# Three more seven-product pairs, and weight sums made in HBM by DMAs, in a two-layer decoder trunk

## The chip, the cores and the metric

The kernel runs on one core of a Trainium2 chip. The time is device microseconds of one execution; the median of several is compared. A core has TensorE (PE; its weight loads are listed apart as PEld), VectorE (DVE), ScalarE (ACT), GpSimd (POOL) and SyncE (SP), which work side by side and wait for each other through semaphores. Loads and stores are DMAs; SP, ACT and POOL can issue them.

## The reference

Two layers on x of 512 tokens by 1024 features, all in float32:

```python
h = rmsnorm(x, g_mix)
aq, ak, av, rq, rk, rv, rg, ga, gb = split(h @ w_in)     # 5888 columns
ya = sliding_window_sink_attention(rope(aq), rope(ak), av, sinks) @ w_a
r = chunkwise_retention(rotate(rq), rotate(rk), rv)
r = r * rsqrt(mean(r * r) + EPS) * silu(rg)              # per head
mixed = sigmoid(ga) * ya + sigmoid(gb) * (r @ w_b)
x = x + mixed @ w_out
x = x + square(relu(rmsnorm(x, g_mlp) @ w_up)) @ w_down  # 1024 -> 4096 -> 1024
```

After both layers a final RMSNorm gives the output. The inputs are drawn at random with fixed seeds.

## The kernel before, in words

**Products.** Activations lie transposed, 128 features by 512 tokens, and each float32 operand is held as a high part and a low part (`split`, L336). A product is three matmuls: high by high, high by low, low by high (L332 to L334). A "chunk" is 128 output features of all tokens; over 1024 input features it takes 8 x 3 = 24 matmuls of 512 columns.

**Weights** come in units of 128 x 1024 in the order of `unit_order` (L59). For each, SP loads the raw unit (`load_until`, L186), ACT copies its high part (L286), DVE takes the low part by subtraction (L287). There are three buffers for raw units and three each for high and low parts; unit i+2 is split when unit i is taken up (`unit`, L292), and loads run some three units ahead of that.

**Pairs.** Two output chunks can be made together in seven products of half the tokens instead of eight (Strassen's scheme in Winograd's form; `narrow_pair`, L629, and, with two of three matmuls merged, `wide_pair`, L1327). A pair is four "parts", each at the size of a unit, that hold the two halves of the weights and four sums of them (S1 to S3 and the like, `add_part`, L248). The activations need four sums as well, the "forms" (`sum_input`, L594: four sums and two splits for each half of the features). A narrow pair works with 256 columns, its three accumulators are copied or joined by ACT and DVE (L640 to L661), and the `step` argument lets other work be placed between its products. In this kernel pairs are w_b 0 and 2 (retention output), w_out 2, 4 and 6, and all of w_up from unit 4 on; w_down is plain, in twos (`two_chunks`, L406), and its last quarter is a `group` of four chunks (L387) and four single chunks (L1446 to L1451).

**Sums of the weights.** For most pairs DVE makes them in place, 4 x 128x512, when the part is due. For the five pairs of `PARKED` (L54) they are made earlier in the same layer, beside w_in's value projection: `raws_ahead` (L230) loads both units, `sums_ahead` (L237) adds and stores four sums to HBM, and `load_part` (L211) later loads the parts ready-made. A pair loads 1 MB when DVE makes the sums and 1.75 MB when they are parked.

**Order.** The code gives each engine's order as a priority; the framework's list scheduler then places ready work first, so that TensorE's order of units can differ a little from the code's. SP and POOL work off their DMAs in the order given.

**Around the change.** In the MLP (`mlp_sequence`, L82), two w_down chunks alternate with one w_up pair. After layer 0's last chunk, `put_down(c, True)` (L1414) adds to x, splits the new input for layer 1 (L342, L343), adds its squares (L425, L426) and stores x to `spill`. Layer 1's first group of w_in begins at once; after its first unit the squares' sum is prepared (L435, L436, L339, L340), and after its second unit TensorE sums them over features and ACT and DVE make the reciprocal RMS (L474 to L477). In the retention output, `mixed_pair` (L1218) multiplies a pair with its gate; chunks 4 to 7 go through `put_mixed` (L1195). `silu` (L976) is a Sigmoid on ACT and a product on DVE; around it ACT also makes Sigmoid gates (L904, L1124) and square roots (L451, L476).

Of the kernel before, what the change touches and what calls it, by code (L numbers as in the profile page):

```python
# [18 lines left out]
P = 128  # L19
T = 512  # L20
# [33 lines left out]
PARKED = (("w_b", 0), ("w_b", 2), ("w_out", 6), ("w_up", 4), ("w_up", 6))  # L54
# [4 lines left out]
def unit_order():  # L59
# [68 lines left out]
def decoder(ctx, tc, xT, x_first, w_in, w_a, w_b, w_out, w_up, w_down, tables, decay, band, triangles, g_last, out):  # L128
# [37 lines left out]
    order = [(layer, *u) for layer in range(DEPTH) for u in unit_order()]  # L166
# [19 lines left out]
    def load_until(n):  # L186
        while state["loaded"] < min(n, len(order)):
# [4 lines left out]
            else:  # L192
                raws[i] = raw_tile()
                for at in halves(i):
                    queue = nc.scalar if i == 0 and at.start == 0 else nc.sync
                    queue.dma_start(raws[i][:, at], weights[name][layer, j][:, at])
                    if i < 3:
                        load_x()
            state["loaded"] += 1

# [5 lines left out]
    park = {at: dram.tile([P, 4, T], F32, name="park_%s_%d" % at) for at in PARKED}  # L206

    def is_parked(i):
        return order[i][1] == "pair" and (order[i][4], order[i][2]) in park

    def load_part(i):  # L211
        layer, _, j, part, src = order[i]
        one, two = (weights[src][layer, j + a] for a in range(2))
        if is_parked(i):
            sums = park[src, j]
            raws[i] = raw_tile()
            sides = ((one[:, LEFT], sums[:, 0, :]), (sums[:, 1, :], one[:, RIGHT]), (sums[:, 2, :], sums[:, 3, :]), (two[:, LEFT],))
            for side, part_of in zip((LEFT, RIGHT), sides[part]):
                nc.sync.dma_start(raws[i][:, side], part_of)
# [17 lines left out]
    def sums_ahead(src, j, two):  # L237
# [4 lines left out]
        nc.vector.tensor_tensor(w2[:, RIGHT], w1[:, LEFT], w2[:, RIGHT], ALU.subtract)  # L242
        nc.vector.tensor_tensor(w1[:, LEFT], s1, w1[:, LEFT], ALU.subtract)
        nc.vector.tensor_tensor(w1[:, RIGHT], w1[:, RIGHT], w1[:, LEFT], ALU.subtract)
        for n, part in enumerate((s1, w1[:, LEFT], w2[:, RIGHT], w1[:, RIGHT])):
            nc.sync.dma_start(park[src, j][:, n, :], part)

    def add_part(i):  # L248
# [4 lines left out]
        elif part == 1:  # L253
            w1 = raws[i - 1]
            nc.vector.tensor_tensor(raws[i][:, LEFT], w1[:, RIGHT], w1[:, LEFT], ALU.subtract)
        elif part == 2:
            raws[i] = big("raw3").rearrange("p a t -> p (a t)")
            w1, w2, z2 = raws[i - 2], raws[i + 1], raws[i - 1]
            nc.vector.tensor_tensor(raws[i][:, LEFT], w1[:, LEFT], w2[:, RIGHT], ALU.subtract)
            nc.vector.tensor_tensor(raws[i][:, RIGHT], z2[:, RIGHT], z2[:, LEFT], ALU.subtract)  # L260
# [320 lines left out]
    def layer_body(layer):  # L581
# [12 lines left out]
        def sum_input(by_form, b, ks):  # L594
# [11 lines left out]
            split(*parts_of_forms(0), f[0].rearrange("p (j k) t -> p j k t", k=2))  # L606
            nc.vector.tensor_tensor(t3, b22, b12, ALU.subtract)
            nc.vector.tensor_tensor(t4, b21, t2, ALU.subtract)
# [20 lines left out]
        def narrow_pair(pool, step, form, block, put):  # L629
# [23 lines left out]
            ins = nc.vector.tensor_tensor(z[:, 1, SECOND], b, eu[:, :H], ALU.add).ins  # L653
# [7 lines left out]
            put(1, FIRST, b, z)  # L661
# [314 lines left out]
        def silu(i):  # L976
            s = temp("sig")
            nc.scalar.activation(s, rg[i], AF.Sigmoid)
            nc.vector.tensor_tensor(rg[i], rg[i], s, ALU.mult)
# [132 lines left out]
        to_load, to_sum = [(layer, *at) for at in PARKED], []  # L1112

        def load_ahead():
            if to_load:
                to_sum.append((*to_load[0][1:], raws_ahead(*to_load.pop(0))))
# [101 lines left out]
        def mixed_pair(c):  # L1218
# [4 lines left out]
            def put(i, at, src, z):  # L1223
# [10 lines left out]
        for c in (0, 2):  # L1234
            mixed_pair(c)
        all_of(delayed)
# [3 lines left out]
        homes_m = [forms_home(), None, forms_home(), None]  # L1240
        by_form_m = [h and h[1] for h in homes_m]
        sum_input(by_form_m, gate_tiles[:2], 0)
        for c in range(4, KD):
# [29 lines left out]
        def add_to_x(c):  # L1273
            def put(i, at, src, z):
                own = x[:, c + i, at] if isinstance(i, int) else x[:, c : c + 2, at]
                return nc.vector.tensor_tensor(own, own, src, ALU.add)
# [21 lines left out]
        def positive(i, at, src, z):  # L1298
# [3 lines left out]
            return nc.vector.scalar_tensor_tensor(z[:, i, at], src, 0.0, factor, ALU.max, ALU.mult)  # L1302
# [5 lines left out]
        up = [[] for _ in range(4)]  # L1308
        up_slots = [[] for _ in range(4)]
# [329 lines left out]
```

## Time and profile before

| | |
|---|---|
| median of 3 runs | 1473.33 us (1473.19 to 1473.95) |
| the profiled execution | 1473.8 us |
| its span, first to last instruction | 1472.0 us |
| moved by DMA | 194.45 MB, mean 132 GB/s |
| read from HBM, written to HBM | 171.63 MB, 18.89 MB |

A busy time is the union of an engine's instructions; matmuls overlap in the pipeline, so their own durations are longer than the distance between their starts. A row of instructions gives its start and its length in us, engine, line, operation and tiles (out<-in), the shape, how many it merges (x), and in brackets what the engine waited for before it. A row of a group gives the count, then busy us and mean ns, then the engine's idle time before. A row of DMAs gives the count, KB each and the median us from issue to landing. "L333" is line 333.

### The profile page before, as it was taken

To read this page: it belongs to the slowest core of one execution; us is meant where nothing else is said; L and a number is where in the kernel's file an instruction comes from. 1 tells how busy PE (TensorE), PEld (TensorE's weight loads), DVE (VectorE), ACT (ScalarE), POOL (GpSimd) and SP (SyncE) were. 2 spreads that over 40 slices of the span, in tenths; PEclk is the share of its full clock that TensorE was granted. 3 is DMA by queue.
4 is the path that set the end of the run, shared out by engine and by line. 5 is a ranking of instruction groups with operands and counts; after the bars stand their busy time and mean duration, and the time that the engine had idled before them with its cause. 6 is when DMAs were issued, how large, how long until landed. Compare 5 with 4: busy or idle time off the path is not lost.

```text
span 1472.0 us, 20220 instructions
## 1 busy us (share of the span) xinstructions
PE 1464.8 (100%) x7466; PEld 1249.6 (85%) x7466; DVE 1166.7 (79%) x1920; ACT 810.9 (55%) x1306; POOL 3.8 (0%) x14
## 2 busy tenths in 40 slices
PE   9999999999999999999999999999999999999998
PEld 7888888888988888888888888888989888888887
DVE  7998878778988787776678986786899877878763
ACT  7656356654684445444455753656547754444553
POOL 0000000000000000000000000000000000000000
PEclk9999999999999999999999999999999999999999
DMA  6422843356443332333543258333654522333241
GB/s 227 127 89 92 300 158 99 102 172 212 126 126 118 101 115 93 104 104 115 165 126 97 86 186 272 104 104 102 207 171 126 154 95 93 114 106 109 90 140 57
DMA packets 71043, 194.45 MB, mean 132 GB/s; under 512 B 8457, under 2 KB 8609, under 8 KB 70945
## 3 DMA queue, kind: packets, MB, share of 16 engines
q1 hardware_dynamic: 70656, 192.65, 40.7%
q8 instruction: 58, 0.95, 0.3%
q10 hardware_dynamic: 288, 0.52, 0.1%
q14 instruction: 41, 0.33, 0.1%
HBM read 171.63 MB, written 18.89 MB: 129 GB/s over the span
## 4 chain that ended last, share of the span: by engine, by line
PE 94%; issue 5%; DMA 1%; DVE 0%; ACT 0%; POOLq 0%; DVEq 0%; SPq 0%
PE mm L334 22%; PE mm L332 22%; PE mm L333 22%; PE mm L1336 11%; PE mm L1337 5%; PE rv L332 2%; PE rv L333 2%; PE rv L334 2%; PE score L842 1%; PE r L332 1%; PE r L334 1%; PE r L333 1%; PE pT L797 0%; PE pv L823 0%; PE pv L824 0%
## 5 line engine op out<-in xcount | busy, mean ns | idle before, releaser
L333 PE MATMUL mm<-r,hi 128*128 128x512 f32 (+1 forms) x1568 | 572.5, 367 | 0.0
L332 PE MATMUL mm<-r,hi 128*128 128x512 f32 (+1 forms) x1568 | 569.7, 367 | 0.6 <-ACT r L342 0.6
L334 PE MATMUL mm<-r,lo 128*128 128x512 f32 (+1 forms) x1568 | 563.9, 367 | 0.2
L286 ACT ACTIVATE hi<-raw 128x1024 fp32r<-128x1024 f32 (+1 forms) x334 | 334.1, 1002 | 386.4 <-PE mm L333 206.8
L287 DVE TENSOR_TENSOR lo<-raw,hi 128x512 fp32r<-128x512 f32 (+1 forms) x335 | 384.7, 1151 | 111.6 <-ACT hi L286 107.9
L334 PEld LDWEIGHTS mm<-r,lo 128*128 128x128 f32 x1568 | 293.7, 188 | 48.7 <-DVE lo L287 1.4
L332 PEld LDWEIGHTS mm<-r,hi 128*128 128x128 f32 x1568 | 293.8, 188 | 47.5 <-ACT r L342 1.4
L333 PEld LDWEIGHTS mm<-r,hi 128*128 128x128 f32 x1568 | 294.3, 188 | 45.9
L1336 PE MATMUL mm<-r,hi 128*128 128x512 f32 x728 | 252.1, 391 | 0.0
L1337 PE MATMUL mm<-r,lo 128*128 128x256 f32 x728 | 200.5, 277 | 0.0
L1336 PEld LDWEIGHTS mm<-r,hi 128*128 128x128 f32 x728 | 136.5, 188 | 28.6
L1337 PEld LDWEIGHTS mm<-r,lo 128*128 128x128 f32 x728 | 136.7, 188 | 3.1 <-DVE lo L287 0.7
L1416 DVE TENSOR_TENSOR x<-x,mm 128x512 f32<-128x512 f32 x56 | 37.8, 686 | 28.9 <-PE mm L334 28.9
L1409 ACT ACTIVATE z<-z 128x512 f32<-128x512 f32 x56 | 32.4, 623 | 48.7 <-DVE z L1389 48.7
L333 PE MATMUL rv<-lo,r 128*128 128x512 f32 x128 | 49.8, 389 | 0.0
L334 PE MATMUL rv<-hi,r 128*128 128x512 f32 x128 | 49.5, 389 | 0.0
L332 PE MATMUL rv<-hi,r 128*128 128x512 f32 x128 | 49.4, 390 | 0.0
L340 DVE TENSOR_TENSOR r<-z,r 128x512 fp32r<-128x512 f32 x64 | 42.9, 686 | 3.0 <-ACT r L339 2.6
L339 ACT ACTIVATE r<-z 128x512 fp32r<-128x512 f32 x64 | 38.4, 619 | 7.9 <-DVE z L1070 7.8
L869 ACT ACTIVATE sm<-sm,st 128x256 f32<-128x256 f32 (+1 forms) x64 | 30.1, 472 | 18.9 <-DVE st L857 18.7
L1389 DVE SCALAR_TENSOR_TENSOR z<-z,rstd 128x512 f32<-128x512 f32 x52 | 35.7, 687 | 0.6
L340 DVE TENSOR_TENSOR r<-sums,r 128x1024 fp32r<-128x1024 f32 x24 | 28.9, 1220 | 0.0
(273 smaller groups left out, 1693.0 us busy)
## 6 DMA issues: line engine op xcount, KB each, us to landing
raw<-w_in_in SPq DMA_DIRECT2D x89, 512.0 KB, 3.7
raw<-w_down_in SPq DMA_DIRECT2D x64, 512.0 KB, 3.6
raw<-w_up_in SPq DMA_DIRECT2D x32, 512.0 KB, 4.0
raw<-w_up_in SPq DMA_DIRECT2D x60, 256.0 KB, 2.9
raw<-w_a_in SPq DMA_DIRECT2D x8, 512.0 KB, 4.8
ahead<-w_b_in SPq DMA_DIRECT2D x8, 512.0 KB, 5.4
park_w_b<-ahead SPq DMA_DIRECT2D x16, 256.0 KB, 5.7
ahead<-w_up_in SPq DMA_DIRECT2D x8, 512.0 KB, 4.9
```

Source lines behind the costliest of these rows:

```text
L286: nc.scalar.activation(hi[:, at], raw[:, at], AF.Copy)
L287: last_low[:] = [nc.vector.tensor_tensor(lo[:, at], raw[:, at], f32(hi[:, at]), ALU.subtract).ins]
L332: nc.tensor.matmul(ps, ah, bh, start=start and i == 0, stop=False, **more)
L333: nc.tensor.matmul(ps, ah, bl, start=False, stop=False, **more)
L334: nc.tensor.matmul(ps, al, bh, start=False, stop=stop and i == n - 1, **more)
L339: nc.scalar.activation(hi, src, AF.Copy)
L340: nc.vector.tensor_tensor(lo, src, f32(hi), ALU.subtract)
L1336: nc.tensor.matmul(both, hi[:, c], m, start=start and k == 0, stop=False, **more)
L1337: nc.tensor.matmul(ps[:, :H], lo[:, c], m[:, 0, :], start=False, stop=k == 3 and start, **more)
L1389: nc.vector.scalar_tensor_tensor(z[:, :, at], z[:, :, at], 0.0, factor, ALU.max, ALU.mult)
L1409: nc.scalar.activation(z[:, i, :], z[:, i, :], AF.Square)
L1416: nc.vector.tensor_tensor(x[:, c, :], x[:, c, :], ps, ALU.add)
```

## The change

- `unit_order` depends on the layer: layer 1 has three pairs of w_b (0, 2, 4) and two chunks; layer 0's last quarter of w_down is four plain chunks as a group and two pairs (w_down 28 and 30). In `last_quarter` the forms of the MLP's activations are made from the quarter's own tiles during the group, its evacuation is spread over the first pair, and the closing work of each chunk over the second pair and after it.
- Layer 0 still parks five pairs through DVE. Layer 1 parks none that way. Instead, twelve pairs' sums are made by DMAs from HBM to HBM while layer 0's MLP runs: w_up 24 to 30 and w_down 28 and 30 of layer 0, then w_b 0, 2, 4, w_out 6 and w_up 4, 6 of layer 1. Each add is two copies issued by SP and two copies and four accumulating DMAs issued by POOL. It is placed behind the load of a unit whose planned start (2.45 us per part of a pair, 5.45 us per plain unit) passes the figure in `BY_DMA`.
- Since a DMA accumulates by adding, the signs of some sums of weights and of forms are turned, so that all four sums of weights are additions; the signs return in the evacuations.
- `silu` is one Silu on ACT.

```diff
-PARKED = (("w_b", 0), ("w_b", 2), ("w_out", 6), ("w_up", 4), ("w_up", 6))
+PARKED = ((("w_b", 0), ("w_b", 2), ("w_out", 6), ("w_up", 4), ("w_up", 6), ), ())
+PAIR_US, PLAIN_US = 2.45, 5.45
+THREE = (1,)
+BY_DMA = (
+    (420.0, 0, ("w_up", 24)),
+    (440.0, 0, ("w_up", 26)),
+    (460.0, 0, ("w_up", 28)),
+    (480.0, 0, ("w_up", 30)),
+    (500.0, 0, ("w_down", 28)),
+    (520.0, 0, ("w_down", 30)),
+    (560.0, 1, ("w_b", 0)),
+    (580.0, 1, ("w_b", 2)),
+    (600.0, 1, ("w_b", 4)),
+    (620.0, 1, ("w_out", 6)),
+    (640.0, 1, ("w_up", 4)),
+    (660.0, 1, ("w_up", 6)),
+)
...
-    order += pairs("w_b", 0, 2) + plain("w_b", 4, 8)
+    order += pairs("w_b", *range(0, paired_rows(layer), 2)) + plain("w_b", paired_rows(layer), 8)
...
+        elif layer == DEPTH - 1:
+            order += plain("w_down", 8 * q, 8 * q + 8)
         else:
-            order += plain("w_down", 8 * q, 8 * q + 8)
+            order += plain("w_down", 8 * q, 8 * q + 4) + pairs("w_down", 8 * q + 4, 8 * q + 6)
...
             state["loaded"] += 1
+            if by_dma and by_dma[0][0] <= starts[i]:
+                with tc.issue_after(last_load[0]):
+                    add_up(*by_dma.pop(0)[1:])
...
+    starts, last_load = [0.0], []
+    for u in order:
+        starts.append(starts[-1] + (PAIR_US if u[1] == "pair" else PLAIN_US))
...
+    def add_up(layer, at):
+
+        src, j = at
+        one, two = (weights[src][layer, j + a] for a in range(2))
+        s = [park[layer, src, j][:, n, :] for n in range(4)]
+        nc.sync.dma_start(s[0], two[:, RIGHT])
+        nc.sync.dma_start(s[2], two[:, RIGHT])
+        nc.gpsimd.dma_start(s[0], two[:, LEFT], accum_op=ALU.add)
+        nc.gpsimd.dma_start(s[2], one[:, LEFT], accum_op=ALU.add)
+        nc.gpsimd.dma_start(s[1], s[0])
+        nc.gpsimd.dma_start(s[1], one[:, LEFT], accum_op=ALU.add)
+        nc.gpsimd.dma_start(s[3], s[1])
+        nc.gpsimd.dma_start(s[3], one[:, RIGHT], accum_op=ALU.add)
...
         def silu(i):
-            s = temp("sig")
-            nc.scalar.activation(s, rg[i], AF.Sigmoid)
-            nc.vector.tensor_tensor(rg[i], rg[i], s, ALU.mult)
+            nc.scalar.activation(rg[i], rg[i], AF.Silu)
...
         for c in (0, 2):
             mixed_pair(c)
+        homes_m = [forms_home(), None, forms_home(), None]
+        by_form_m = [h and h[1] for h in homes_m]
+        delayed.append(partial(sum_input, by_form_m, gate_tiles[:2], 0))
+        if layer in THREE:
+            mixed_pair(4)
         all_of(delayed)
...
+        def last_quarter(q):
+            new_input()
+            homes_u = [forms_home() for _ in range(4)]
+            by_form_u = [h[1] for h in homes_u]
...
+            def sum_up(ks):
+                early, (_, _, late) = up_tiles[q][ks // 2 :: 2]
+                whole = big("up")
+                nc.vector.tensor_tensor(whole, f32(early[0]), f32(early[1]), ALU.add)
+                sum_input(by_form_u, [whole, late], ks)
+
+            def close(c):
+                scaled_input(c, g_mix + 2)
+                squared_input(c, g_mix + 2)
+                nc.sync.dma_start(spill[:, c, :], x[:, c, :])
...
+                def step(ins):
+                    if next(turn) in (0, 2, 4) and waiting:
+                        with tc.issue_after(ins):
+                            waiting.pop(0)()
...
+            evacuates = [put_down(c) for c in range(4)]
+            waiting.extend(group("w_down", layer, up[q], evacuates, {0: partial(sum_up, 0), 1: partial(sum_up, 2)}))
+            for c in (4, 6):
+                narrow_pair(ps_aux if c == 4 else ps_mm, spread(), form_of(by_form_u), block_u, add_to_x(c))
+                if c == 4:
+                    all_of(waiting)
+                    waiting[:] = [partial(close, c) for c in range(4)]
+                waiting.extend(partial(close, c + i) for i in range(2))
+            all_of(waiting)
...
-                all_of(group("w_down", layer, up[q], [put_down(c, True) for c in range(4)]))
-                for c in range(4, KD):
-                    chunk("w_down", layer, up[q], put_down(c, True))
-                slots.give(*up_slots[q])
+                last_quarter(q)
```

More of the change, by code (lines that the diff above doesn't have):

```diff
@@ L163, in decoder @@
     spill, aside = (dram.tile([P, KD, T], F32, name=n) for n in ("spill", "aside"))
-    order = [(layer, *u) for layer in range(DEPTH) for u in unit_order()]
+    order = [(layer, *u) for layer in range(DEPTH) for u in unit_order(layer)]
     raws, parts, homes = {}, {}, []
@@ L195, in load_until @@
                     queue = nc.scalar if i == 0 and at.start == 0 else nc.sync
-                    queue.dma_start(raws[i][:, at], weights[name][layer, j][:, at])
+                    load = queue.dma_start(raws[i][:, at], weights[name][layer, j][:, at]).ins
+                    if queue is nc.sync:
+                        last_load[:] = [load]
                     if i < 3:
@@ L214, in load_part @@
         if is_parked(i):
-            sums = park[src, j]
+            sums = park[layer, src, j]
             raws[i] = raw_tile()
@@ L235, in raws_ahead, with sums_ahead @@
         return two
-    def sums_ahead(src, j, two):
+    def sums_ahead(at, two):
         w1, w2 = two
@@ L1239, in layer_body @@
             slots.give(*t[1])
-        homes_m = [forms_home(), None, forms_home(), None]
-        by_form_m = [h and h[1] for h in homes_m]
-        sum_input(by_form_m, gate_tiles[:2], 0)
-        for c in range(4, KD):
+        for c in range(paired_rows(layer), KD):
             if c % 2 == 0:
@@ L1308, in layer_body @@
         up = [[] for _ in range(4)]
+        up_tiles = [[] for _ in range(4)]
         up_slots = [[] for _ in range(4)]
```

93 lines of the change are left out of this document (57 added, 36 removed).

## The prediction

> **What bounds the kernel now.** I read the page's busy times first, then the chain of waits, then stages.
>
> ```profile
> span 1472.0 us, 20220 instructions
> PE 1464.8 (100%) x7466; PEld 1249.6 (85%) x7466; DVE 1166.7 (79%) x1920; ACT 810.9 (55%) x1306; POOL 3.8 (0%) x14
> PE 94%; issue 5%; DMA 1%; DVE 0%; ACT 0%; POOLq 0%; DVEq 0%; SPq 0%
> ```
>
> PE (TensorE) is busy for 1464.8 of 1472.0 us and carries the chain. So removed VectorE (DVE) work or earlier transfers buy almost nothing alone: only fewer PE-microseconds, or a PE wait removed, shorten the span. POOL is free.
>
> A busy PE says little of one matmul, since their spans overlap. The pitch is the distance of starts (TensorE's timeline where retention output begins):
>
> ```profile
> 318.81 0.39 PE L332 MATMUL mm<-r,hi 128*128 128x512 f32 x1
> 319.04 0.39 PE L333 MATMUL mm<-r,hi 128*128 128x512 f32 x1
> ...
> 319.61 0.28 PE L332 MATMUL mm<-r,hi 128*128 128x256 f32 x1
> ...
> 320.55 0.28 PE L334 MATMUL mm<-r,lo 128*128 128x256 f32 x1
> ```
>
> A 512-column matmul takes about 0.23 us of PE, and eight 256-column ones 0.94 us, 0.1175 each: a little over half.
>
> ```profile
> 319.50:341.30 21.80, 21.80 (x171) 21.14 (x170) 15.92 (x22) 11.26 (x17) 0.00 (x0) 1.00 0.80 264
> 362.90:402.70 39.80, 39.71 (x289) 37.33 (x288) 36.64 (x55) 25.16 (x39) 0.00 (x0) 1.00 0.39 118
> 577.00:597.50 20.50, 20.50 (x105) 17.46 (x104) 15.86 (x25) 10.16 (x15) 0.00 (x0) 1.00 0.30 105
> 697.00:734.70 37.70, 37.70 (x168) 31.21 (x167) 24.45 (x32) 18.78 (x28) 0.00 (x0) 1.00 0.49 161
> 734.70:745.60 10.90, 10.90 (x49) 9.01 (x48) 5.77 (x7) 4.43 (x7) 0.00 (x0) 1.00 0.44 145
> 1047.60:1069.40 21.80, 21.80 (x171) 21.14 (x170) 15.96 (x22) 11.26 (x17) 0.00 (x0) 1.00 0.83 276
> ```
>
> These rows give length, then busy PE, PEld, DVE, ACT and POOL, clock, DMA share, GB/s. The stages are retention output (both layers), w_out, one MLP cycle, layer 0's last quarter, and layer 1's first two units. The clock is 1.00. Only w_out lacks PE time, and there DVE is 92% busy.
>
> **The pairs.** L640 occurs once per narrow pair:
>
> ```profile
> L332 PE MATMUL mm<-r,hi 128*128 128x256 f32 x336 | 93.4, 279 | 0.0
> L640 ACT ACTIVATE mm<-mm 128x256 f32<-128x256 f32 x12 | 4.4, 368 | 9.5 <-PE mm L334 9.5
> 729.26 0.69 DVE L1416 TENSOR_TENSOR x<-x,mm 128x512 f32<-128x512 f32 x1 [2.03 <-PE mm L334]
> 734.70 0.69 DVE L1416 TENSOR_TENSOR x<-x,mm 128x512 f32<-128x512 f32 x1 [2.04 <-PE mm L334]
> ```
>
> 336/12 = 28 matmuls on each of three lines: 84 per pair, 84 x 0.1175 = 9.87 us. Two plain chunks take 2 x (734.70 - 729.26) = 10.88 us. A pair saves 1.01 us; the change makes three: layer 0's w_down 28 and 30, layer 1's w_b 4. **-3.03 us**. It removes no other matmul.
>
> **Layer 0's last quarter** pays on DVE. Durations:
>
> ```profile
> L287 DVE TENSOR_TENSOR lo<-raw,hi 128x1024 fp32r<-128x1024 f32 x291 | 355.1, 1221 | 105.8 <-ACT hi L286 102.1 <-PE mm L334 1.9 <-DMA ahead<-w_up_in 0.2
> L340 DVE TENSOR_TENSOR r<-sums,r 128x1024 fp32r<-128x1024 f32 x24 | 28.9, 1220 | 0.0
> L605 DVE TENSOR_TENSOR sums<-gate,sums 128x512 f32<-128x512 f32 x4 | 2.7, 687 | 0.1
> L653 DVE TENSOR_TENSOR z<-mm,eu 128x256 f32<-128x256 f32 x12 | 5.1, 421 | 1.2 <-PE mm L334 1.0
> ```
>
> Added: `sum_up` twice, one 128x1024 sum, four sums like L605, two splits like L340: 2 x (1.22 + 2.75 + 2.44) = 12.8 us. Eight pair parts are split instead of four units: 6 x 1.22 + 2 x 0.69 - 4 x 1.22 = 3.8. Evacuation: per pair four 256-column operations and a 512-column one, 2.37, for two L1416: 2 x 2.37 - 4 x 0.69 = 2.0. Together 18.6 on the 24.45 us of row 697-734.7: 43.0 us of DVE in 35.7 us of PE. Some 7.4 us spill into layer 1's w_in, beside 5.77 in its first 10.9. The spilled part is mostly squares and splits of late chunks, which PE needs units later. Bounds: 0 if the spill hides; 7.4 + 5.77 - 10.9 = 2.3 us if the RMS matmul, put after two units, waits for it. The nearest row is w_out's crowded DVE, and its waits in the chain are these (the longer):
>
> ```profile
> 380.71 0.39 PE mm L334
> ...
> 391.10 1.23 DVE lo L287
> 392.38 0.38 PE mm L334
> ```
>
> A weight split (L287) stands behind other DVE work, and the piece of PE that follows it takes 0.38 us where 0.12 is the pitch; with the one at 380.71 this is 2 x 0.27, some 0.55 us in all, at 92% of DVE. Here DVE is asked for more than all of the time, and parts of it can slide: I take **+0.7 us**, nearer that row than the 2.3.
>
> **DMA-made sums.** They take 20 ahead-sums of layer 1 and the in-place sums of w_up 24 to 30 off DVE (0.69 each): hidden behind PE, worth 0. They remove layer 1's ahead loads and parked stores and add, per pair, two SP copies and six POOL DMAs of 256 KB. A parked load is 1.75 MB per pair, an unparked one 1 MB. The retention rows show parked pairs at DMA shares 0.80 and 0.83 with PE filled: I cost layer 1's third one at 0 (no gain, since the stage has no PE wait to remove; at most 2.7 us, the extra 0.75 MB at the 276 GB/s of that row, if nothing of it is ahead of time).
>
> Is a sum ready, and what does it disturb?
>
> ```profile
> raw<-w_up_in SPq DMA_DIRECT2D x32, 512.0 KB, 4.0
> raw<-park_w_up SPq DMA_DIRECT2D x16, 256.0 KB, 4.1
> park_w_up<-ahead SPq DMA_DIRECT2D x16, 256.0 KB, 7.3
> spill<-x SPq DMA_DIRECT2D x8, 256.0 KB, 2.1
> 450.78 0.33 SPq L196 DMA_DIRECT2D raw<-w_down_in  x1
> 692.06 0.33 SPq L196 DMA_DIRECT2D raw<-w_down_in  x1
> ...
> 699.28 5.79 SPq L196 DMA_DIRECT2D raw<-w_down_in  x3
> ```
>
> By the unit order the first add follows the load of w_down 3 (450.78); the others follow about one MLP cycle apart, in the order of use. The pair at w_down 28 is loaded from 692.06 on, the one at 30 within the row at 699.28. POOL issues one DMA after the other and waits where it needs the last one's bytes. So six adds, 36 POOL DMAs taken as a row, must end by about 700: (700 - 451)/36 = 6.9 us each. No row shows a DMA from HBM to HBM, or one that accumulates; the ends are 2.1 (a write to HBM) and 7.3 (stores issued four in a row), and I take 4.1, a read of HBM of that size: 25 us per add, the sixth done at 451 + 36 x 4.1 = 599. Cost 0; layer 1 needs its six sums 300 us later.
>
> Slack of the weights beside them, in an MLP cycle:
>
> ```profile
> 590.20 0.69 DVE L252 TENSOR_TENSOR raw<-raw 128x512 f32<-128x512 f32 x1
> 593.60 1.23 DVE L287 TENSOR_TENSOR lo<-raw,hi 128x1024 fp32r<-128x1024 f32 x1 [0.78 <-ACT hi L286]
> 599.33 0.40 PE L1336 MATMUL mm<-r,hi 128*128 128x512 f32 x1
> ```
>
> L252 at 590.20 is the first to touch the pair's last load; the split of its first part ends at 594.83, and PE wants that part at 599.33. The load may land 4.5 us later at no cost. The adds move 2 MB per cycle of 20.5 us, 102 GB/s beside the 105 of row 577-597.5: 207, under the 264 to 276 that retention bears with PE full; counted twice, as they read and write HBM, 309. Cost 0: nothing to gain, as no matmul there waits for a transfer, and up to rival C to lose.
>
> **Silu** replaces a Sigmoid and L979's product:
>
> ```profile
> L979 DVE TENSOR_TENSOR z<-z,sig 128x512 f32<-128x512 f32 x16 | 10.7, 686 | 3.5 <-ACT sig L978 3.5
> L904 ACT ACT_TABLE_LOAD x4 | 5.1, 1283 | 0.1
> ```
>
> DVE loses 10.7 us where no matmul waits for it: nothing gained. Silu and Sigmoid alternate with each other in two places of a layer; if each place costs ACT a table load of 1.28 us, that is 5.1 us. ACT is 55% busy and PE is full there, which hides it: 0, and 5.1 us without that cover.
>
> **Sum.** -3.03 + 0.7 = -2.3. The profiled execution took 1473.8 us, 1.8 outside its span, so 1471.5; it stood 0.5 above the median of the runs, 1473.33, which becomes **1471.0**.
>
> **Rivals.**
> *A, no new wait*: the spill hides, or freed DVE time removes one w_out wait: -3.0 to -3.9, 1469.4 to 1470.3. For it: row 734.70-745.60 leaves 5.1 of 10.9 us of DVE idle, which can take most of the spill. Against: the w_out pairs that wait today stay unparked.
> *B, the last quarter is DVE-bound*: the RMS matmul waits the whole 2.3 us and two weight splits 0.6 each: -3.03 + 3.5, 1473.8. For it: 43.0 us in 35.7.
> *C, slower, the adds crowd the weights*: from a landing 4.5 us late on, each of twelve add cycles stalls PE; 0.5 us each is 6 us, net +3, 1476.3; 1.5 us each 18, 1488. The two copies also stand in SP's own queue ahead of the next weight load. The rule is in the Trainium skill, "DMA: Bandwidth & Descriptors", section "Issuing engines are not separate DMA queues": DMAs of any issuer share the same 16 engines and interleave. The row at share 0.80 agrees that sharing is borne there.
> *D, the sums come late*: over 6.9 us per POOL DMA, SP stops at the parked load, and every weight load behind it. At the 7.3 of the parked stores, 451 + 36 x 7.3 = 714, 14 us late, about 10 past the slack: 1481.
> *E, the change does less than it says*: the pairs' later parts wait for their evacuations, so that 84 matmuls take as long as 48 plain ones: 1473.3 to 1474. Retention's pairs speak against it.
>
> **How the numbers follow.** Forecast (waits of 0 to 1.5 us, 1470.3 to 1471.8) 0.50, a fifth of it under 1470.4; A 0.14; B 0.11; E 0.05; C 0.14; D 0.06. A measurement of this kernel tells about 0.2% (2.95 us) from no change: faster is under 1470.4, A and the forecast's low part, 0.25; slower is over 1476.3, C and D, 0.20; the rest, 0.55, is no change. The range from 1469.7 reaches into C, to 1477.0; what lies out is D, C's upper half and A's end. C's low end decides its top.
>
> **What would show it.** L332 with 256 columns should count 252 more over three lines, 512 columns 144 fewer; the span's PE busy should fall by about 3 us. Right: no PE wait between 440 and 700, parked landings near 4 us. Wrong: a gap of PE over 1 us near 745 (B), landings of w_up or w_down over 8 us (C), SP waiting before a parked load near 600 to 700 (D).

## The result, and the profile after

The changed kernel takes **1514.35 us** (median of 5 runs, 1503.35 to 1521.4) where the kernel before takes 1473.33 (5 runs beside them, 1473.08 to 1475.53): 1.027 of the time before, 95% interval 1.0229 to 1.0311, **slower by 41 us**. The forecast was 1471.0 with a range to 1477.0. The profiled execution is the slowest of the five: 1521.4 us, of which 1519.6 are its span, 47.6 more than the span before. In the code of the changed kernel the lines have moved: L332 to L334 (a pair's and a chunk's matmuls) are L379 to L381, the wide matmuls L1386 and L1387, the splits L333 and L334, the in-place sums L299 to L306, SP's loads L218, L270, L272 and L275, an add's POOL transfers L251 to L256.

The top of the page, its queues, and the chain by engine:

```profile
span 1519.6 us, 20578 instructions
PE 1482.9 (98%) x7574; PEld 1262.9 (83%) x7574; DVE 1153.1 (76%) x1896; ACT 826.9 (54%) x1329; POOL 56.8 (4%) x86
q1 hardware_dynamic: 74256, 193.96, 39.6%
q0 software_dynamic: 8832, 18.88, 8.8%
PE 80%; DMA 7%; issue 6%; DVE 4%; ACT 3%; POOLq 0%; SPq 0%; ACTq 0%; DVEq 0%
```

PE held 94% of the chain before and holds 80% now. DMA, DVE and ACT have come into it: PE waits. Its busy time is 18.1 us longer although the matmuls cost less, so it also ran slower. Where, is read from equal windows of both kernels (length, then busy PE, PEld, DVE, ACT, POOL, the granted clock, DMA share, GB/s). Before:

```profile
480.00:620.00 140.00, 140.00 (x712) 119.27 (x712) 108.17 (x165) 67.37 (x101) 0.00 (x0) 1.00 0.33 108
620.00:690.00 70.00, 70.00 (x358) 59.72 (x358) 54.61 (x84) 35.11 (x53) 0.96 (x1) 1.00 0.30 96
690.00:730.00 40.00, 40.00 (x180) 33.16 (x179) 24.60 (x34) 18.10 (x26) 0.00 (x0) 1.00 0.51 169
730.00:800.00 70.00, 70.00 (x327) 58.23 (x326) 55.40 (x124) 40.38 (x87) 0.00 (x0) 1.00 0.40 121
```

After:

```profile
480.00:620.00 140.00, 121.91 (x558) 100.39 (x557) 83.87 (x131) 52.70 (x78) 21.82 (x30) 0.93 0.72 155
620.00:690.00 70.00, 70.00 (x352) 59.21 (x351) 47.18 (x71) 32.31 (x47) 10.36 (x14) 1.00 0.79 194
690.00:730.00 40.00, 35.26 (x171) 28.75 (x171) 22.52 (x36) 17.85 (x27) 5.16 (x8) 0.96 0.84 204
730.00:800.00 70.00, 64.81 (x352) 56.07 (x351) 51.09 (x68) 34.62 (x50) 11.79 (x16) 0.95 0.86 218
```

PE is idle for 18.1 + 0 + 4.7 + 5.2 = 28.0 us, and it works at a mean clock under 1, worth about 0.07 x 121.9 + 0.04 x 35.3 + 0.05 x 64.8 = 13 us more: 41 of the 47.6. The starts of the matmuls give a finer count, since a row's busy time covers small gaps: the distance from one start to the next, less the pitch of that size in the kernel before. By them gaps and slower pitch take some 46 us between 480 and 800 us, where the adds run, and 2.4 us more than before in layer 1's w_out. So nearly all of the loss lies where the adds run. Read the last two columns against each other: before, retention moved 264 GB/s at a DMA share of 0.80; here 0.72 moves 155. The engines are as busy and move little more than half. The view of the DMAs says which transfers they are busy with (KB each, median us from issue to landing):

```profile
raw<-w_up_in SPq DMA_DIRECT2D x28, 512.0 KB, 4.0
sums_w_up<-w_up_in POOLq DMA_DIRECT2D x24, 256.0 KB, 8.9
sums_w_up<-sums_w_up POOLq DMA_DIRECT2D x12, 256.0 KB, 5.0
```

The second row are accumulating DMAs, the third plain copies of the same size and issuer. The median of a weight load, 4.0, hides the late ones, since most loads have no add beside them. One cycle shows one. POOL's timeline:

```profile
501.92 0.56 POOL L255 DMA_DIRECT2D sums_w_up<-sums_w_up  x1 [4.38 <-DMA sums_w_up<-w_up_in]
506.56 0.80 POOL L256 DMA_DIRECT2D sums_w_up<-w_up_in  x1 [4.09 <-DMA sums_w_up<-sums_w_up]
507.10 1.10 POOL L251 DMA_DIRECT2D sums_w_up<-w_up_in  x1
507.63 1.40 POOL L252 DMA_DIRECT2D sums_w_up<-w_up_in  x1
```

The last transfer of one add (L256) and the first two of the next (L251, L252) are issued within 1.1 us: three accumulating DMAs at once, which land 9.5 to 12.5 us later (516.07 to 520.15). Earlier on this timeline the add before starts at 479.56, so adds follow each other after 27.5 us: as long as one takes, and more than the 20.5 of a cycle before. So they run one into the other. The chain beside it:

```profile
510.99 10.02 DMA raw<-w_up_in
521.02 0.70 DVE raw L299
...
524.12 1.22 DVE lo L334
525.34 0.35 DVE z L1391
525.71 0.70 DVE z L1445
...
529.16 0.79 PE mm L1386
```

The weight load issued at 510.99 lands 10.02 us later, past any slack; sum, split and the evacuation behind it on DVE are late, and then PE is:

```profile
526.82 0.28 PE L1387 MATMUL mm<-r,lo 128*128 128x256 f32 x1
529.16 0.79 PE L1386 MATMUL mm<-r,hi 128*128 128x512 f32 x1 [2.06 <-ACT mm L1419]
529.75 0.41 PE L1387 MATMUL mm<-r,lo 128*128 128x256 f32 x1
529.96 0.63 PE L1386 MATMUL mm<-r,hi 128*128 128x512 f32 x1
```

Behind the gap a 512-column matmul takes 0.43 us of PE (529.96 to 530.39) in place of 0.23. The clock is the reason:

```profile
529.20:532.40 3.20, 3.20 (x10) 2.72 (x11) 2.68 (x5) 2.28 (x4) 0.42 (x1) 0.50 0.86 229
```

Half the clock for some 3 us behind each such gap.

### The profile page after: what moved, and what is told of

Its sections match the earlier page's. It is cut to its first block, busy times and chain, and to the rows that moved or that the text cites. A ratio compares the mean times of both kernels' runs of the same rounds, so it can differ in the third digit from the quotient of the medians.

```text
span 1519.6 us, 20578 instructions
## 1 busy us (share of the span) xinstructions
PE 1482.9 (98%) x7574; PEld 1262.9 (83%) x7574; DVE 1153.1 (76%) x1896; ACT 826.9 (54%) x1329; POOL 56.8 (4%) x86
## 3 DMA queue, kind: packets, MB, share of 16 engines
q0 software_dynamic: 8832, 18.88, 8.8%
## 4 chain that ended last, share of the span: by engine, by line
PE 80%; DMA 7%; issue 6%; DVE 4%; ACT 3%; POOLq 0%; SPq 0%; ACTq 0%; DVEq 0%
PE mm L381 19%; PE mm L379 19%; PE mm L380 19%; PE mm L1386 9%; PE mm L1387 4%; DMA raw<-w_up_in 3%; DVE lo L334 2%; DMA raw<-w_down_in 2%; PE rv L379 2%; PE rv L381 2%; PE rv L380 2%; ACT hi L333 1%; DMA raw<-w_in_in 1%; PE score L889 1%; DMA raw<-w_b_in 1%
## 5 line engine op out<-in xcount | busy, mean ns | idle before, releaser
L379 PE MATMUL mm<-r,hi 128*128 128x512 f32 (+1 forms) x1604 | 577.2, 364 | 7.8 <-ACT hi L333 6.6
L380 PE MATMUL mm<-r,hi 128*128 128x512 f32 (+1 forms) x1604 | 580.1, 363 | 0.0
L381 PE MATMUL mm<-r,lo 128*128 128x512 f32 (+1 forms) x1604 | 570.5, 364 | 1.4 <-DVE lo L334 1.2
L333 ACT ACTIVATE hi<-raw 128x1024 fp32r<-128x1024 f32 (+1 forms) x340 | 338.8, 999 | 410.7 <-PE mm L380 170.2
L334 DVE TENSOR_TENSOR lo<-raw,hi 128x512 fp32r<-128x512 f32 (+1 forms) x341 | 389.5, 1146 | 135.3 <-ACT hi L333 133.9
L379 PEld LDWEIGHTS mm<-r,hi 128*128 128x128 f32 x1604 | 302.0, 189 | 55.1 <-ACT hi L333 7.5
L381 PEld LDWEIGHTS mm<-r,lo 128*128 128x128 f32 x1604 | 301.2, 188 | 50.8 <-DVE lo L334 4.7
L380 PEld LDWEIGHTS mm<-r,hi 128*128 128x128 f32 x1604 | 302.2, 189 | 44.6
L1386 PE MATMUL mm<-r,hi 128*128 128x512 f32 x728 | 262.7, 402 | 15.9 <-ACT mm L1419 13.1
L1387 PE MATMUL mm<-r,lo 128*128 128x256 f32 x728 | 205.6, 284 | 4.1 <-DVE lo L334 4.0
L1386 PEld LDWEIGHTS mm<-r,hi 128*128 128x128 f32 x728 | 141.0, 194 | 48.9 <-ACT mm L1419 14.9
L1387 PEld LDWEIGHTS mm<-r,lo 128*128 128x128 f32 x728 | 141.1, 194 | 9.0 <-DVE lo L334 6.7
L381 PE MATMUL rv<-hi,r 128*128 128x512 f32 x128 | 49.8, 389 | 0.0
L379 PE MATMUL rv<-hi,r 128*128 128x512 f32 x128 | 49.8, 390 | 0.0
L299 DVE TENSOR_TENSOR raw<-raw 128x512 f32<-128x512 f32 x24 | 16.6, 691 | 42.7 <-DMA raw<-w_up_in 41.7
L1473 DVE TENSOR_TENSOR x<-x,mm 128x512 f32<-128x512 f32 x52 | 34.6, 684 | 18.3 <-PE mm L381 18.2
```

What stands on the lines that cost most here:

```text
L333: nc.scalar.activation(hi[:, at], raw[:, at], AF.Copy)
L334: last_low[:] = [nc.vector.tensor_tensor(lo[:, at], raw[:, at], f32(hi[:, at]), ALU.subtract).ins]
L379: nc.tensor.matmul(ps, ah, bh, start=start and i == 0, stop=False, **more)
L380: nc.tensor.matmul(ps, ah, bl, start=False, stop=False, **more)
L381: nc.tensor.matmul(ps, al, bh, start=False, stop=stop and i == n - 1, **more)
L1386: nc.tensor.matmul(both, hi[:, c], m, start=start and k == 0, stop=False, **more)
```

## The experiments

Medians are compared with the kernel before as run on the same chip beside them (1472.6 to 1473.0). An add is two copies by SP and six transfers by POOL, of which four accumulate and two copy: 48 accumulating DMAs in all, not the 36 that two of the expectations name.

**Which part costs.** First the adds by themselves, put into the kernel before:

```
 kernel before
+            if by_dma and by_dma[0][0] <= starts[i]:
+                with tc.issue_after(last_load[0]):
+                    add_up(*by_dma.pop(0)[1:])
...
```

> The kernel before, with only the twelve adds put in at the places of the change; their sums go to tiles that nobody reads, and everything else is as before. Theory (the adds slow the weight loads that run beside them, from 3.5 us to 10 us, PE waits, and its clock is lower after each wait): nearly all of the loss is here, 1473 + 30 to 50 = 1503 to 1523, with weight landings over 8 us and PE gaps between 480 and 800 us. Rival (the pairs, the crowded DVE of the last quarter or the late start of layer 1 make the loss): at most 3 us over the kernel before, 1473 to 1476.

1499.95 us (1496.65 to 1503.08), ratio 1.0183 [1.0167, 1.0199]: +27.3. The theory's first case, a little under its range. Its windows:

```profile
480.00:620.00 140.00, 128.95 (x629) 107.30 (x628) 95.44 (x146) 60.18 (x90) 22.91 (x32) 0.98 0.73 167
620.00:690.00 70.00, 63.66 (x298) 52.39 (x296) 45.55 (x70) 27.97 (x42) 13.31 (x18) 0.95 0.83 186
690.00:730.00 40.00, 39.53 (x195) 33.09 (x196) 23.91 (x39) 16.05 (x24) 4.99 (x7) 1.00 0.76 170
```

PE idles 11.1 and 6.3 us in the first two windows and hardly in the third, where the changed kernel idles 4.7: there the adds meet the changed last quarter, whose pairs load parked sums too. By the starts of matmuls PE loses 16 us between 690 and 800 us in the changed kernel and 1.4 here, so most of the other 14 us stand there. That this meeting makes them is argued; no run shows it alone.

The other way round, the changed kernel without the adds (stand_ins are halves of the weight for a sum that a DMA would make, and the parked sums for the others):

```
-            if by_dma and by_dma[0][0] <= starts[i]:
-                with tc.issue_after(last_load[0]):
-                    add_up(*by_dma.pop(0)[1:])
...
-            sides = ((one[:, LEFT], sums[:, 0, :]), (sums[:, 1, :], one[:, RIGHT]), (sums[:, 2, :], sums[:, 3, :]), (two[:, LEFT],))
+            sides = ((one[:, LEFT], stand_ins[0]), (stand_ins[1], one[:, RIGHT]), (stand_ins[2], stand_ins[3]), (two[:, LEFT],))
```

> The changed kernel without the twelve adds: where a sum would be loaded, half of the weight itself is loaded in its place, of the same size, so every other load, DVE operation and matmul is the changed kernel's, and the outputs are not the reference's (the sums are left out). Theory (the adds alone cost): the pairs keep their gain, 3.03 us less PE, and the last quarter costs 0 to 1.5 us: 1470 to 1472. Rival (the pairs or the last quarter's DVE work cost as well): 1474 or more, with a gap of PE near 745 us.

1472.55 us (11 runs), ratio 0.9999 [0.999, 1.0008]. The rest of the change costs nothing, but it gains nothing that can be measured either: both expectations are missed by half a microsecond or more. Its waits of PE in layer 0's last quarter and the next stage, then in layer 1's w_out:

```profile
PE mm L381 <- DVE z L702: 0.5, 1, 0.5
PE mm L381 <- DVE z L1019: 0.3, 1, 0.3
```

```profile
PE mm L381 <- ACT eu L692: 0.3, 1, 0.3
PE mm L383 <- DVE lo L336: 0.2, 1, 0.2
```

This view lists none for the kernel before in these windows; by the starts of matmuls it loses 0.6 us in that w_out, and this run 1.3. The third pair's own stage, retention output (1040 to 1090 us), shows no lost time in either. Three of the four stand in a pair, the first in a new one of w_down, the last two in pairs of w_out that both kernels have: a later part waits for the evacuation of an earlier one (z L702, eu L692) or for its own split (lo L336).

The copies that SP issues, and Silu, each alone in the kernel before:

```
 add_up of the adds alone, in the kernel before
         nc.sync.dma_start(s[0], two[:, RIGHT])
         nc.sync.dma_start(s[2], two[:, RIGHT])
-        nc.gpsimd.dma_start(s[0], two[:, LEFT], accum_op=ALU.add)
...
-        nc.gpsimd.dma_start(s[3], one[:, RIGHT], accum_op=ALU.add)
```

> The kernel before with only the 24 copies that SP issues for the adds, in the places of the change, and none of POOL's DMAs; nobody reads them. Theory (POOL's DMAs make the loss): within 0.2% of the kernel before. Rival (the copies stand in SP's queue ahead of the next weight load and make it late): half or more of the 27 us that the adds alone cost, 1486 or more.

1472.84 us in one run, beside 1472.85. SP's queue is not the cause.

```
-            s = temp("sig")
-            nc.scalar.activation(s, rg[i], AF.Sigmoid)
-            nc.vector.tensor_tensor(rg[i], rg[i], s, ALU.mult)
+            nc.scalar.activation(rg[i], rg[i], AF.Silu)
```

> The kernel before with Silu in place of Sigmoid and its product, and nothing else. Prediction: within 0.1% of the kernel before, since ACT's table loads are hidden behind PE. Rival (the table loads stand in front of weight splits that PE waits for): up to 5.1 us slower.

1473.02 us (10 runs), ratio 1.0 [0.9991, 1.001]. As predicted.

**What of an add costs.** The four accumulating DMAs of each add as copies (the first of them is shown):

```
-        nc.gpsimd.dma_start(s[0], two[:, LEFT], accum_op=ALU.add)
+        nc.gpsimd.dma_start(s[0], two[:, LEFT])
```

> The changed kernel with its 36 accumulating DMAs as plain copies of the same size, queue and order; the sums are left out, so the outputs are not the reference's. Theory 1 (what counts is how many transfers are under way, of any kind): 1495 or more. Theory 2 (an accumulating packet holds an engine longer than a copied one, 0.24 us for 2 KB over POOL's queue, and this is what the weights wait for): the packets of POOL's queue fall to about 0.13 us each, the weight loads beside them land within 6 us, and the time is 1472 to 1482.

1474.5 us in one run, 1.7 over the kernel before. Same queue, same order, same bytes by the page: 39 us of the 41 are gone. So it is the accumulating, and theory 1 as it stood (any transfers at once) falls. Three of POOL's transfers were under way at once here too, but between 440 and 830 us for 24 us in place of 69, as copies land sooner. So this run does not part the longer hold on the engines from the longer overlap that it brings. Weight loads in that stretch landed within 6.5 us, but for one of 8.1. Its queue, its transfers and its window:

```profile
q0 software_dynamic: 5760, 18.88, 5.0%
sums_w_up<-w_up_in POOLq DMA_DIRECT2D x24, 256.0 KB, 4.7
480.00:620.00 140.00, 140.00 (x712) 119.08 (x711) 105.00 (x161) 67.65 (x101) 17.77 (x34) 1.00 0.67 194
```

More GB/s than in the changed kernel (194 against 155), and PE full. From the queue rows: a copy is 5760/72 = 80 packets and 0.050 x 16 x 1472.7/72 = 16.4 us of engine time. An accumulating DMA is (8832 - 24 x 80)/48 = 144 packets and (0.088 x 16 x 1519.6 - 24 x 16.4)/48 = 36.4 us. That is 2.2 times the copy; by q1's row in the changed kernel, 49.6 us per MB, 256 KB of weights take 13.0. Theory 2's figure was off in its form: a copied packet is 0.20 us, not 0.13, but there are fewer of them.

Is it the number of accumulating DMAs, or how many run at once? Third sum last, so that at most two do:

```
-        nc.sync.dma_start(s[2], two[:, RIGHT])
...
         nc.gpsimd.dma_start(s[3], one[:, RIGHT], accum_op=ALU.add)
+        nc.gpsimd.dma_start(s[2], two[:, RIGHT])
+        nc.gpsimd.dma_start(s[2], one[:, LEFT], accum_op=ALU.add)
```

> The changed kernel with the add's third sum made last and its copy issued by POOL, so that at most two of POOL's DMAs are under way at once in place of three; bytes and places are the same, 36 accumulating DMAs included. Theory 1 (three at once make the weight loads late): the loss falls to a third or less, 1475 to 1490. Theory 2 (the bytes, or the engine time of accumulating packets, count, however they are ordered): 1500 to 1525 still.

1493.76 us (1492.71 to 1497.53), ratio 1.015 [1.0134, 1.0165]. This doesn't test what it was made for: with no wait on SP's copy left, POOL issued all twelve third sums in the first 31 us. The first 40 us of this run and of the kernel before:

```profile
0.00:40.00 40.00, 29.17 (x105) 22.51 (x106) 18.55 (x28) 19.30 (x31) 18.18 (x36) 0.87 1.01 300
```

```profile
0.00:40.00 40.00, 38.33 (x159) 31.05 (x160) 30.02 (x41) 26.49 (x42) 1.92 (x12) 1.00 0.62 209
```

At a DMA share of 1.01 PE lost 9.2 us, and some 0.13 x 29 = 4 more by its clock: 13 of the 21.

> As the run with the adds in turn, and spread out: five adds stand in layer 0's first stage (nominal starts 60, 100, 205, 235 and 270 us) and seven in the MLP 40 us apart in place of 20. Theory (an add longer than its cycle of 20.5 us runs into the next one, and this crowds the weights): with 40 us for each the waits go, 1470 to 1474. Rival (each add stalls PE by itself): still 2 to 4 us per add, 1495 or more.

1491.27 us, ratio 1.0125 [1.0111, 1.0138], with the same loss at the start (diff: the start times only). In the MLP, where now one accumulating DMA at a time runs, nothing is lost:

```profile
480.00:620.00 140.00, 140.00 (x709) 119.01 (x708) 108.72 (x164) 68.11 (x102) 12.76 (x18) 1.00 0.54 141
```

The third sums held in place:

```
+        last = nc.gpsimd.dma_start(s[3], one[:, RIGHT], accum_op=ALU.add).ins
+        with tc.issue_after(last):
+            last = nc.gpsimd.dma_start(s[2], two[:, RIGHT]).ins
+            with tc.issue_after(last):
+                nc.gpsimd.dma_start(s[2], one[:, LEFT], accum_op=ALU.add)
```

> The changed kernel with each add's third sum made behind the fourth, both of its transfers on POOL, and (other than in the run with the adds in turn, where POOL issued them all in the first 31 us) held there by the order of issue: at most two of POOL's DMAs under way at once, 84 in all, 20 us from add to add as in the change. Theory 1 (three at once make the weight loads late): the MLP before its last quarter loses 0 to 3 us in place of 24 to 42, 1472 to 1478. Theory 2 (bytes and accumulating packets count, in whatever order): 1490 or more, since the bytes are the change's plus one copy per add.

1537.00 us (median of 1534.97, 1537.00 and 1539.18; one more execution took 1816.83), ratio 1.0436 [1.0415, 1.0457], slower than the change. Both theories are out, for a reason that neither had:

```profile
ACT r L800 <- POOL r L740: 63.0, 1, 63.0
...
PEld score L888 <- ACT r L800: 56.5, 1, 56.5
```

L740 is a memset of layer 1's value tile, issued on POOL. POOL works in order, the last transfer of the adds was issued at 839 us, the memset stood behind it (839.9), and PE waited 56 us for it. In the changed kernel the same memset runs at 798.9, early enough that no wait names it. Moved to DVE:

```
-        nc.gpsimd.memset(f32(v_t[:, 2:4, :]), 0.0)
+        nc.vector.memset(f32(v_t[:, 2:4, :]), 0.0)
```

> The run that made the adds' third sums last, with layer 1's zeroing of the value tile moved from POOL, where it stood behind the adds until 840 us, to DVE. Theory 1 (two accumulating DMAs at once do little, three make the loss, and the 63 us that ACT waited for POOL's memset was a loss of its own): 1473 to 1480. Theory 2 (accumulating packets cost the same in any order): 1490 or more.

1482.69 us (1480.3 to 1493.11), ratio 1.0082 [1.0052, 1.0112]: +9.7, between the two theories. With all 48 accumulating DMAs and one copy more per add, three quarters of the loss are gone; so the order counts, but not alone. Half of the accumulating DMAs, once apart and once together:

```
 chain_adds: accum_op only for s[1] and s[3], which wait for each other
 twin_adds:  accum_op only for s[0] and s[2], which are issued together
```

> The changed kernel with two of the four accumulating DMAs of each add (the second and the fourth sum, issued one after the other's landing) kept, and the other two, which are issued together, as plain copies: 24 accumulating DMAs, hardly ever two at once. Order, queue and bytes are the change's; those sums are left out, so the outputs are not the reference's. Theory 1 (the loss comes from accumulating DMAs that run at once): at most 5 us over the run with plain copies, 1474 to 1480. Theory 2 (each accumulating DMA costs its share): half of the 41 us, near 1494, and the same as the run of the twin adds.

> The mirror of the run of the chain adds: the two accumulating DMAs of each add that are issued together (first and third sum) are kept, the other two are plain copies. Again 24 accumulating DMAs, with two at once; the sums of the plain ones are left out. Theory 1 (at once): clearly more than the chain adds, 1480 to 1495. Theory 2 (each its share): the same as the chain adds, near 1494.

1487.13 us (1483.83 to 1494.55), ratio 1.0103 [1.0071, 1.0134], and 1484.3 (1478.57 to 1499.61), ratio 1.0084 [1.0048, 1.012]. They can't be told apart, against theory 1; but half of the accumulating DMAs cost 14 and 11 us where all of them cost 41 in one order and 10 in another, against theory 2. What fits all of them, though no run shows it alone, is a threshold: a load costs nothing until it lands later than its slack. Between 440 and 830 us, weight loads of 256 and 512 KB with on average none, one and two accumulating DMAs beside them landed in 4.0, 5.2 and 8.3 us in the changed kernel (medians of 10, 9 and 10 loads, longest 6.0, 9.1 and 13.5; two loads had three beside them), against 3.6 before (longest 4.2). With the 4.5 us of slack that the prediction read for one load of the cycle, only the landings over 8 us would count. Last, the sums in place and memset on DVE, with the adds spaced out (diff: the start times 60, 100, 205, 245, 285, 420, 460, 500, 540, 580, 620, 660):

> The run with the memset on DVE, with the adds spaced out: five in layer 0's first stage (nominal starts 60, 100, 205, 245 and 285 us) and seven in the MLP, 40 us or more apart, so that an add of seven POOL transfers (about 35 us) ends before the next one starts. All twelve sums are made by DMA, as in the change. Theory (a weight load that lands within the 4.5 us of slack costs nothing, and only loads beside two or more accumulating DMAs land later): no gap of PE over 1 us, 1472 to 1475. Rival (each accumulating DMA costs its share, as the 24 of the chain adds and of the twin adds seemed to, 0.5 us each): 1490 or more.

1480.16 us (1477.19 to 1483.08), ratio 1.0045 [1.0033, 1.0057]. Not 1490: between 440 and 700 us PE has no wait at all. But the forecast of no gap is missed too. The waits that remain are in the stages that were tight already, in retention output and w_out, then in the last quarter:

```profile
PE mm L383 <- DVE lo L336: 1.4, 3, 0.7
PE mm L382 <- DVE r L389: 1.2, 1, 1.2
PE mm L381 <- ACT hi L335: 1.0, 1, 1.0
```

```profile
PE mm L381 <- ACT mm L689: 1.4, 1, 1.4
PE mm L381 <- ACT eu L692: 1.1, 1, 1.1
```

The fifth add, planned for 285 us, was issued from 329 to 365 us, in retention output and w_out, and DVE carries the memset in the last quarter.

**The clock.** A wait of PE made without any DMA, by repeating three weight splits in the kernel before:

```
+AGAIN = {(0, "w_down", 4): 7, (0, "w_down", 12): 10, (0, "w_down", 18): 13}
-                last_low[:] = [nc.vector.tensor_tensor(lo[:, at], raw[:, at], f32(hi[:, at]), ALU.subtract).ins]
+                for _ in range(AGAIN.get(order[i], 0) + 1):
+                    last_low[:] = [nc.vector.tensor_tensor(lo[:, at], raw[:, at], f32(hi[:, at]), ALU.subtract).ins]
```

> The kernel before with one weight split in each of three places of layer 0's MLP written 8, 11 and 14 times over in place of once (the result is the same), so that PE waits for it with no DMA beside it: DVE loses 8.5, 12.2 and 15.9 us there, of which 4.5 us and what DVE idles are hidden. Theory (PE's clock is lower for some 4 us after any wait of PE of some microseconds): behind each gap of PE over 1 us the pitch of 512 columns goes from 0.23 to 0.43 us for 3 to 4 us, so that the span grows by the gaps plus 1.5 to 2 us for each. Rival (the lower clock comes with the load of the DMA engines): the pitch behind the gaps stays 0.23 us, and the span grows by the gaps alone.

1520.34 us in one run, +47.5 for 36.6 us of DVE work. A stretch without a gap, and one behind the first three gaps (3.6, 1.4 and 1.6 us of idle):

```profile
470.00:484.00 14.00, 14.00 (x75) 11.92 (x74) 11.40 (x17) 8.96 (x14) 0.00 (x0) 1.00 0.22 75
497.20:499.50 2.30, 2.30 (x9) 1.91 (x9) 2.27 (x3) 1.73 (x4) 0.00 (x0) 0.50 0.44 169
```

The clock halves behind the gaps with the DMA share at 0.44, so the gaps do it and not the load of the DMA engines. By the starts of its matmuls, 13 gaps make 31.5 us and the slower pitch some 15 more, 1.2 us per gap: under the 1.5 to 2 that was expected, because several gaps share one slow stretch (the clock's record has 5 for the 13 gaps).

**The pairs.** Layer 0's two pairs alone, summed by DVE, and then the third pair with them (there THREE stays (1,)):

```
+BY_DMA = ()
+PARKED = ((("w_b", 0), ("w_b", 2), ("w_out", 6), ("w_up", 4), ("w_up", 6)),) * 2
+THREE = ()
```

> The changed kernel without DMA-made sums and without the third pair of retention output: layer 1's five parked pairs are summed ahead by DVE as before, and w_up 24 to 30 and w_down 28 and 30 are summed in place by DVE. What is left of the change is layer 0's two pairs and Silu. Theory (pairs gain 1.01 us each, the last quarter gives 0.7 to 1.5 back): 1471.3 to 1472.3 where the kernel before takes 1472.8. Rival (with the in-place sums DVE bounds the last quarter): 1473.5 or more, with gaps of PE between 700 and 760 us.

> As the run before this one, with the third pair of retention output in layer 1 as well, its sums made in place by DVE. Theory (the pair gains 1.01 us, and since only 1 MB is loaded for it in place of 1.75 MB, no wait of the third pair appears): 1.0 us under that run. Rival (the third pair's first parts wait, as for 1 to 2 us near 1085 us in the run of the pairs without adds): the same as that run or slower.

1472.86 us (11 runs), ratio 0.9999 [0.999, 1.0009], and 1476.53 (7 runs), ratio 1.0026 [1.0015, 1.0036]. Two pairs gain nothing, and the third, with its sums made in place, loses 3.7 us where a gain of 1.0 was expected. In layer 1's retention output of the latter, PE waits:

```profile
PE mm L368 <- DVE lo L321: 1.6, 1, 1.6
PE mm L366 <- DVE z L687: 1.5, 1, 1.5
```

With parked sums it has no wait there (the run without adds), so the third pair needs them. The rival came true; the theory's reason, that fewer bytes are loaded, did not count. The wait near 1085 us that the rival takes from the run without adds is not in that run's trace. Is DVE's load the reason in the last quarter? Two variants sum pairs of w_down ahead in the first stage:

```
 ahead5: PARKED[0] has ("w_down", 28), ("w_down", 30) in place of ("w_up", 4), ("w_up", 6)
 ahead6: PARKED[0] has ("w_down", 28) as well, summed beside the third w_a chunk
```

> As the run by DVE with layer 0's two pairs, but layer 0 sums those two pairs ahead, in its first stage, in place of w_up 4 and 6. Theory (the pairs lose their gain to waits in the last quarter because DVE is full there): the 5.5 us of sums that leave DVE there take the waits of 0.5 and 0.9 us at 717 and 759 us away, 1471 to 1472. Rival (w_up 4 and 6, summed in place again, wait at the start of the MLP): 1473 or more.

> As the run by DVE with layer 0's two pairs, but the first of them is summed ahead too, as a sixth pair of layer 0's first stage, at the place between its third and fourth w_a chunk. Theory: half of the last quarter's sums leave DVE, 1471.3 to 1472.3, a little under the run by DVE. Rival (the sixth pair's loads and sums cost in the first stage what they save later): 1472.9 or more.

1472.55 us (11 runs), ratio 0.9999 [0.999, 1.0007], and 1481.86 (5 runs), ratio 1.0059 [1.0045, 1.0073]. Taking the sums off DVE recovers nothing, and a sixth pair ahead costs 9 us, most of it in the first stage (5.9 us of waits between 160 and 200 us, by starts of matmuls). No version is measurably faster than the kernel before.

## Why the prediction was wrong, by its steps

- **The step that failed** is "Slack of the weights beside them": 102 GB/s of adds beside 105 makes 207, "under the 264 to 276 that retention bears with PE full", "Cost 0". Bytes per second were the wrong measure. An accumulating DMA holds the engines 36.4 us for 256 KB where weights take 13.0, and 155 GB/s of this mix filled the engines to 0.72, as much as some 240 of retention's. The adds cost 27.3 us alone and 41 in the change. Shown by: adds alone, plain copies, SP's copies alone.
- **The duration of a POOL transfer**, 4.1 us from reads of HBM, bounds 2.1 and 7.3: in the changed kernel plain copies took 4.0 to 5.0, accumulating ones 7.7 to 10.5 (medians), outside the bounds. The one row for both kinds was the mistake: 24 of the six adds' 36 transfers accumulate. The sixth add ended at 618, not 599, long before SP loads the first sums of w_down (732): rival D did not come.
- **Rival C** was the mechanism, with chance 0.14 and 0.5 to 1.5 us per add. Its threshold (a landing 4.5 us late) fits the landings. Its price was too low: 41/12 = 3.4 us per add, since landings ran to 13.5 us and adds became longer than a cycle, and each gap over 2 us also halves the clock, which no rival had.
- **The pairs**: 84 matmuls per pair came as counted (1192 of 512 columns per line in place of 1232, 412 of 256 in place of 336, the rest of both under another operand name). -3.03 us of PE follows from these counts. New waits of 0.8 us in the last quarter, 0.6 in the next stage and 0.6 in layer 1's w_out, counted by starts of matmuls, leave -1.0; measured without adds is -0.1, interval -1.5 to 1.2. Rival E (pairs wait for their own evacuations) came true for 0.8 of the 2.0 of layer 0's two pairs; the third pair has no wait in its own stage.
- **Last quarter, +0.7** (bounds 0 to 2.3): 0.8 in the changed kernel without adds. The size agrees by luck, for the cause is another: the waits are for a pair's own evacuations, not for the RMS matmul (rival B) or weight splits, and without DVE's sums they stay.
- **Layer 1's third pair, 0** (at most 2.7): no wait in retention output; w_out behind it lost 0.6, which the prediction had no term for. **Silu, 0**: right. ACT made six more table loads, 7.7 us, hidden as said.

## What to carry to other kernels

Count a transfer by the engine time of its packets, from the queue rows (share x 16 x span / transfers), and not by its bytes: a DMA that accumulates in HBM took over twice a copy's. Ask of background DMAs how many run at once beside a load with little slack, and whether one round of them fits into the cycle that issues the next, for the loss starts at the slack and then grows fast. Look at what else stands in the queue of an idle engine before giving it a long chain of waits: one memset behind POOL's adds cost 56 us.

## What the runs showed of the hardware

A gap of PE of a little over 2 us halved its clock for some 3 us (2.06 us of idle before 529.16); two gaps of 1.5 and 1.6 us close together did not. Those are the two waits of the run by DVE with the third pair; the stretch behind the second:

```profile
1070.80:1073.00 2.20, 2.11 (x18) 2.12 (x19) 2.20 (x5) 1.33 (x2) 0.00 (x0) 1.00 0.52 164
```

The Trainium skill, "TensorE: Matmul & The Clock Gate", section "Part 1: The HAM clock gate (the "warmup" mystery)", has PE at half clock after an idle window of about 3.4 us, until it has been busy for about as long. The traces agree on half and on the length of the slow stretch; 2.06 us of idle were enough here, so the measurement decides that a gap shorter than that window can do it. The clock's records in the traces say more. In the changed kernel its half-clock stretches begin at 505.31, 529.20, 549.68, 583.82 and 611.12 us, whole multiples of 3.41 us apart, and last 3.41 or 6.83 us. In all the runs, each step of such a grid at full clock that held 2.0 us of PE idle or more was followed by half clock, and none that held under 1.5; between the two both occurred. So the idle time within one step counts, not the length of a gap alone.

Unexpected too: the time of the changed kernel varied by 18 us from run to run (1503.35 to 1521.4) where the kernel before varies by 2.5. That its loads land at the edge of their slack may be why; no run tests it.

Left open are the law by which landings grow with the accumulating DMAs beside them, and why the adds cost some 14 us more beside the changed last quarter. A deeper prefetch of weights, which would test the slack directly, was not tried.
